# Attention's per-head steps at fixed distances, all gates of branch A in pairs, and seven projection tiles of branch B behind the last head

## The chip, the cores and the metric

The kernel runs on one core of one Trainium2 chip. Its engines are named in the profile as PE (TensorE matmul) with PEld (TensorE weight load), DVE (VectorE), ACT (ScalarE), POOL (GpSimd) and SP (SyncE, which here only issues DMA transfers). The metric is the device time of one execution in microseconds (us), lower is better; several runs are taken and the median is compared. Profiles come from one further execution.

## The reference, cut to what matters

One layer for 512 frames of width 2048, all in float32. Two mixers share one projection of the normalised input; their outputs are projected, gated and summed.

```python
h = rmsnorm(x, norm_gain)
proj = h @ w_in
(aq, ak, av, az, iq, ik, iw, rq, rk, rv, rz, ga, gb) = jnp.split(proj, SPLIT_POINTS, axis=-1)
...
a_out = dsa_mixer(aq, ak, av, iq, ik, iw, positions, rel_bias) * jax.nn.silu(az)
...
b_out = retention_mixer(rq, rk, rv, ret_gn_gain) * jax.nn.silu(rz)
merged = jax.nn.sigmoid(ga) * (a_out @ w_a_out) + jax.nn.sigmoid(gb) * (b_out @ w_b_out)
r = x + merged @ w_o
return r + (p_i @ w_ple) * jax.nn.sigmoid(r @ w_ple_gate)
```

Mixer A is attention of 8 heads of 128 channels, in which each frame sees a chosen set of up to 128 keys and a bias by distance. Mixer B is a retention of 8 heads. The widths of `az` and `rz` are 1024 each (8 tiles of 128 channels), those of `ga` and `gb` 2048 each (16 tiles).

## The kernel before

**Numbers in two parts.** TensorE multiplies float32 operands rounded to a shorter form (`fp32r`). To keep float32 accuracy every operand is split into a high part and the rest: ScalarE rounds (`wh`, `hh`, `akh`: L138, L386, L673), VectorE or GpSimd subtracts (`wl`, `hl`, `akl`: L144, L387, L674). A product is then three matmuls, high by high, high by low, low by high (`gemms`, L198 to L200). Channels lie on the 128 partitions, the 512 frames along the free axis.

**Steps.** The order of the work is written out by hand. TensorE's program is a chain of steps, one `step()` behind each group of matmuls (three in `gemms` and `values`, two in `gemm_pair`). All other work is queued to be emitted at a step: `later(n, f)` puts `f` n steps ahead of the present one; `todo` is a list of which one entry is taken at each step, in order, so that what is added to a list that is not yet empty comes later; `bg` is background work, of which one entry is taken at every `rate`-th step in which `todo` gives nothing. Each engine executes its own instructions in the order in which they are emitted, and waits in that order.

**Weights.** Each block of 8 rows of 128 weights is a unit: loaded by SP into one of 7 `wraw` buffers (L117), rounded by ScalarE (`wh`), subtracted (`wl`). `split_to` is called at the first step of a unit and emits the splits of units up to 3 ahead, `load_to` the loads of units up to 8 ahead. `pool_units` (L330, L331) lists the ranges of units of which GpSimd instead of VectorE makes `wl`; the second covers attention from its first head to the end of the single gate tiles.

**Pairs.** `gemm_pair` makes two tiles of 128 output channels at once, from 7 products of half size instead of 8 (`PRODUCTS`, L213). Its inputs are 56 prepared tiles `Xh`, loaded from DRAM. A product of a pair is 8 steps of one matmul of 512 and one of 256 columns, so a pair is 56 steps of two matmuls. `gate_pair` applies the gate's function and stores the result.

**Stages around the change**, in order: retention; pairs for `rz` (4), `gb` (8), `ga` (8) and the first four heads of `az` (2, `AZ_PAIRED`); during the last of these B's gated output is loaded and split into `bparts` (`b_load`, L882), from 20 empty steps on, one head every four steps. Then 16 tiles of branch B's output projection (L902 to L907), gated and stored in `mbs`, during which x is loaded again and split into `hparts` (`x_again`). Then attention: a values projection (`values`, 64 steps) ahead of heads 0 and 4, and for each head a queries tile and a keys tile of 16 steps each. Then four single gate tiles (`gated`, L1028) for heads 4 to 7, and branch A's output projection (L1043 to L1053), which needs `aparts`, the gated heads in two parts.

**A head** (`attention_head`, L913) loads its bias and adds the mask on GpSimd at its start (`bm`, L916, L917), projects queries and keys and splits them, and puts the rest on `todo`: the split of the values, four `logits` steps (matmuls, then VectorE adds the bias and takes the maximum), `exps` on ScalarE, `normalize` on VectorE, eight `turn` steps of two 32x320 transposes each on VectorE (L709), two `turn` steps of ScalarE (`pth`, L976) and two of VectorE (`ptl`, L978), and four `outs` steps of matmuls (L992), after which ScalarE copies the head's output `oT`. This list has 38 entries, and a head's two tiles have 32 steps. Heads 0 to 3 are gated during heads 4 to 7 (`a_kept`, L1008).

**Memory.** Tiles of 128 x 512 come from 65 slots (`U`), those of 128 x 1280 (`bm`, `pn`, `pth`, `ptl` among them) from 5 (`B`). A new tile takes the slot that has been free longest and waits for that slot's last reader.

Of the kernel before, what the change touches and what calls it, by code (L numbers as in the profile page):

```python
# [34 lines left out]
def block_kernel(tc, xT, pT, posb, posq, w_in, w_v, w_ik, w_a, w_b, w_o, w_ple, w_gate,  # L35
# [4 lines left out]
    with contextlib.ExitStack() as ctx:  # L40
# [39 lines left out]
        def block(src, chunks, cols=128):  # L80
            ids, k0 = [], 0
            for nk in chunks:
                ids.append(len(units))
                units.append((raw(src, k0, nk, cols), None, nk, cols))
                k0 += nk
            return ids

        def block_pair(s1, s2):

            b11, b12, b21, b22 = (s1, 0), (s2, 0), (s1, 8), (s2, 8)
            first = len(units)
# [83 lines left out]
        def drain():  # L177
            while todo or soon:
                step()
# [135 lines left out]
        u_rz = [block_pair(col(RZ, h), col(RZ, h + 1)) for h in range(0, NH, 2)]  # L315
        u_gb = [block_pair(col(GB, m), col(GB, m + 1)) for m in range(0, 16, 2)]
        u_ga = [block_pair(col(GA, m), col(GA, m + 1)) for m in range(0, 16, 2)]
        u_az = [block_pair(col(AZ, h), col(AZ, h + 1)) for h in range(0, AZ_PAIRED, 2)]
        u_wb = [block(w_b[m], (8,)) for m in range(16)]
        u_a, u_av = [], []  # L320
        for h in range(NH):
            if h % 4 == 0:
                u_av.append(block(w_v[2 + h // 4], (2,) * 8, 512))
            u_a.append([block(col(g, h), K8) for g in (AQ, AK)])
        u_az += [block(col(AZ, h), K8) for h in range(AZ_PAIRED, NH)]
        PAIRED = [m + 8 * i for m in range(8) for i in range(2)]
        u_wa = {m: block(w_a[m], (8,)) for m in PAIRED}
        u_d = [block_pair(w_o[m], w_o[m + 8]) for m in range(8)]
        u_p = [block(w_ple[:, 8 * q:8 * q + 8], (8,)) for q in range(MF // 4)]
        pool_units.append((u_r[0][0][0] + 4, u_r[-1][1][-1] + 1))  # L330
        pool_units.append((u_a[0][0][0] + 4, u_a[-1][1][-1] + 9))  # L331
        u_e = [block(w_gate[m], K8) for m in range(MF)]
        u_t = block(w_gt[0], (2,) * 4 + (1,) * 8, 512), block(w_pt[0], (1, 1), 512)

# [334 lines left out]
        def split(src, name, lag=0):  # L669

            h = U(name + "h", F32R)
            l = U(name + "l", F32R)
            later(lag, lambda: act.activation(h, src, AF.Copy))  # L673
            later(lag and lag + 1, lambda: dve.tensor_sub(l, src, h.bitcast(F32)))  # L674
            return h, l
# [201 lines left out]
        for us, dst in ((u_gb, sgb), (u_ga, sga)):  # L877
            for n, u in enumerate(us):
                gate_pair(u, AF.Sigmoid, to(dst[2 * n:2 * n + 2]))
        bparts = []  # L880

        def b_load(h):  # L882
            t = U("bk")
            sp.dma_start(t, bd[h])
            later(4, lambda: bparts.append(split(t, "b")))

        for n in range(AZ_PAIRED // 2):
            if n == AZ_PAIRED // 2 - 1:
                todo.extend([None] * 20)
                for h in range(NH):  # L890
                    todo.extend([lambda h=h: b_load(h)] + [None] * 3)
            gate_pair(u_az[n], AF.Silu, to(zd[2 * n:2 * n + 2]))
# [6 lines left out]

        state["rate"] = 2  # L900
        todo.extend([f for k in range(KT) for f in (lambda k=k: x_again(k), None, None, None)])
        for m in range(16):  # L902
            s = U("sg")
            sp.dma_start(s, sgb[m])
            pw = gemm(u_wb[m], bparts, "ps_w")
            dve.tensor_mul(s, pw, s)
            later(4, lambda m=m, s=s: sp.dma_start(mbs[m], s))  # L907
        drain()


        oTs = []

        def attention_head(h, vs):  # L913
            hc = slice(128 * (h % 4), 128 * (h % 4) + 128)
            bm = B("bm")
            sp.dma_start(bm, scr[h])  # L916
            pool.tensor_add(bm, bm, mneg)  # L917
            ps = gemm(u_a[h][0], hparts, "ps_aq")
            q = U("aq")
            dve.scalar_tensor_tensor(q, ps, 128.0 ** -0.5, R["b"], op0=OP.mult, op1=OP.mult)  # L920
            qs = split(q, "aq", 1)
            ps = gemm(u_a[h][1], hparts, "ps_ak")
            k = U("ak")
            dve.tensor_mul(k, ps, R["b"])
            ks = split(k, "ak", 1)
            mx = S("mx", 4)
            sums = S("sums", 4)
            E = {}

            def logits(t):  # L930
                ln = 128 * (t + 1)
# [51 lines left out]
            def outs(n):  # L983
                if n == 0:
                    E["po"] = P("ps_o")
                po = E["po"]
                for i in range(3 * n, min(3 * n + 3, len(seq))):
                    a, b, j = seq[i]
                    if j == NT - 1:
                        pe.matmul(po[:, 384:], vs[j][:, hc], bm[:, 896:1024], start=False, stop=False)  # L990
                    else:
                        pe.matmul(po[:, 128 * j:], E["v"][a][:, tok(j)], E["p"][b][:, JOFF[j]:JOFF[j] + L - 128 * j],  # L992
                                  start=(i == 0), stop=(i == len(seq) - 1))
                if n == 3:
                    oT = U("oT")
                    act.activation(oT, po, AF.Copy)
                    oTs.append(oT)
# [8 lines left out]
        aparts = [None] * NH  # L1006

        def a_kept(h):  # L1008
            z = U("z")
            sp.dma_start(z, zd[h])  # L1010
            later(24, lambda: dve.tensor_mul(z, z, oTs[h]))

            def parts():
                aparts[h] = split(z, "a")

            later(25, parts)

        for h in range(NH):
            if h % 4 == 0:
                state["rate"] = 1  # L1020
                av = values(u_av[h // 4], "av")
                while bg:
                    bg.popleft()()
            if h >= NH - AZ_PAIRED:
                a_kept(h - NH + AZ_PAIRED)
            attention_head(h, av)

        def gated(uz, o):  # L1028
            ps = gemm(uz, hparts, "ps_z")
            z = U("z")  # L1030
# [233 lines left out]
AHEAD = 4  # L1264
LOADS = 5
BG_RATE = 3
BG_RATE2 = 24
X_AHEAD = 10
AZ_PAIRED = 4
WARM = 10  # L1270
MANUAL = True

# [95 lines left out]
```

## Time and profile before

| | us |
|---|---|
| median of 3 runs | 1810.67 |
| lowest and highest of them | 1810.29, 1814.06 |
| the profiled execution, its own time | 1809.38 |
| its span, from the first to the last instruction | 1807.6 |

Its granted TensorE clock is 0.990 of full speed over the span. In the profile a row of a group or a timeline names the line, the engine, the operation and `out<-in` by the program's names, then shapes and a count. The idle time shown beside it is that of the same engine just ahead of the instruction, with the instruction that ended it. Where each stage lies, by the first start of its matmuls:

| stage | from, us |
|---|---|
| pairs of gates | 404.1 |
| 16 tiles of branch B's projection | 874.0 |
| values projection, then heads 0 to 3 | 973.0, 1026.8 |
| values projection, then heads 4 to 7 | 1128.9, 1178.3 |
| four single gate tiles | 1284.9 |
| 16 tiles of branch A's projection | 1346.6 |
| pairs of the last projection, w_o | 1433.7 |

### The profile page before, as it was taken

Reading aid. Unit: us, or ns where it says so; the run is one execution under the profiler, and the core shown is the slowest. Engines: PE = TensorE matmul, PEld = TensorE weight load, DVE = VectorE, ACT = ScalarE, POOL = GpSimd, SP = SyncE. Lnnn points to the kernel's source line nnn. Section 1 sums busy time; section 2 is a strip of 40 time slices with the busy share of each in tenths; the row PEclk is TensorE's granted clock in tenths of the full one; section 3 lists DMA queues with packets and bytes.
Section 4 is the critical chain, followed back from the end, with each engine's and each line's share of the span. In section 5 each row is a group of like instructions: output and inputs, shape, how many; then the busy total and the mean of one; then the engine's idle time right before and its main releaser. Section 6 shows DMA issues by size and latency. Waiting matters only on the chain. (4 is left out here: it accounts for less than half of the span.)

```text
span 1807.6 us, 23881 instructions
## 1 busy us (share of the span) xinstructions
PE 1752.1 (97%) x8966; PEld 1462.5 (81%) x8966; DVE 1210.6 (67%) x1959; ACT 738.1 (41%) x1087; POOL 395.4 (22%) x262
## 2 busy tenths in 40 slices
PE   9999999998999999999999999998989999999997
PEld 7988788887888888888777777886778888878887
DVE  8787874867776667776765357547557878774453
ACT  7464332224444545444532333333334443463332
POOL 2002344432321111110000144354310011111222
PEclk9999999999999999999999999999999999999999
DMA  7327652389878877778875423333236578753312
GB/s 280 110 101 265 227 189 98 102 286 290 231 196 208 209 201 206 201 198 202 295 251 178 135 96 104 106 108 117 71 107 206 161 212 205 174 175 105 94 59 93
DMA packets 114580, 309.65 MB, mean 171 GB/s; under 512 B 12832, under 2 KB 21024, under 8 KB 114464
## 3 DMA queue, kind: packets, MB, share of 16 engines
q1 hardware_dynamic: 91072, 244.15, 40.1%
q0 software_dynamic: 13600, 49.29, 14.7%
q10 hardware_dynamic: 9792, 14.68, 2.4%
q8 instruction: 70, 1.15, 0.3%
q14 instruction: 46, 0.38, 0.1%
HBM read 266.14 MB, written 41.94 MB: 170 GB/s over the span
## 5 line engine op out<-in xcount | busy, mean ns | idle before, releaser
L138 ACT ACTIVATE wh<-wraw 128x1024 fp32r<-128x1024 f32 (+2 forms) x404 | 415.5, 1043 | 535.3 <-issue 100.0
L144 DVE TENSOR_TENSOR wl<-wraw,wh 128x1024 fp32r<-128x1024 f32 (+2 forms) x324 | 401.7, 1243 | 258.7 <-ACT wh L138 258.3
L144 POOL TENSOR_TENSOR wl<-wraw,wh 128x1024 fp32r<-128x1024 f32 x80 | 192.6, 2410 | 339.8 <-ACT wh L138 243.2
L106 POOL DMA_DIRECT2D wraw<-w_in x66 | 58.9, 955 | 366.9 <-DVE wl L144 255.3
L253 PE MATMUL ps_r<-hs,wh 128*128 128x512 f32 x352 | 127.9, 402 | 3.7 <-DVE e_d L232 3.4
L694 PE MATMUL ps_vn<-wh,hh 128*128 128x512 f32 x256 | 102.1, 399 | 0.0
L695 PE MATMUL ps_vn<-wl,hh 128*128 128x512 f32 x256 | 100.1, 391 | 0.0
L696 PE MATMUL ps_vn<-wh,hl 128*128 128x512 f32 x256 | 99.8, 390 | 0.0
L254 PE MATMUL ps_r<-hs,wl 128*128 128x256 f32 x352 | 99.0, 281 | 0.2 <-DVE wl L144 0.2
L253 PEld LDWEIGHTS ps_r<-hs,wh 128*128 128x128 f32 x352 | 66.0, 188 | 23.9 <-issue 8.2
L198 PE MATMUL ps_pg<-rh,wh 128*128 128x512 f32 x192 | 74.7, 389 | 0.0
L199 PE MATMUL ps_pg<-rl,wh 128*128 128x512 f32 x192 | 74.7, 389 | 0.0
L200 PE MATMUL ps_pg<-rh,wl 128*128 128x512 f32 x192 | 74.7, 389 | 0.0
L254 PEld LDWEIGHTS ps_r<-hs,wl 128*128 128x128 f32 x352 | 66.5, 189 | 1.1 <-DVE wl L144 1.0
L106 POOL DMA_DIRECT2D wraw<-w_o x24 | 21.1, 933 | 206.8 <-DVE wl L144 179.2
L709 DVE STREAM_TRANSPOSE bm<-pn 32x320 f32<-32x320 f32 x128 | 64.3, 503 | 1.9
L253 PE MATMUL ps_v<-hs,wh 128*128 128x512 f32 x176 | 65.0, 407 | 0.0
L253 PE MATMUL ps_v<-ha,wh 128*128 128x512 f32 x176 | 63.7, 397 | 0.0
L253 PE MATMUL ps_q<-ha,wh 128*128 128x512 f32 x176 | 63.3, 399 | 0.0
L253 PE MATMUL ps_p<-hs,wh 128*128 128x512 f32 x176 | 63.3, 398 | 0.0
L253 PE MATMUL ps_p<-ha,wh 128*128 128x512 f32 x176 | 63.3, 399 | 0.0
L917 POOL TENSOR_TENSOR bm<-bm,mneg 128x1280 f32<-128x1280 f32 x8 | 21.7, 2708 | 182.1 <-DMA bm<-scr 182.1
(389 smaller groups left out, 4709.3 us busy)
## 6 DMA issues: line engine op xcount, KB each, us to landing
wraw<-w_in SPq DMA_DIRECT2D x174, 512.0 KB, 4.4
wraw<-w_in POOLq DMA_DIRECT2D x66, 512.0 KB, 7.9
wraw<-w_v SPq DMA_DIRECT2D x32, 512.0 KB, 3.9
wraw<-w_o SPq DMA_DIRECT2D x32, 512.0 KB, 4.3
wraw<-w_o POOLq DMA_DIRECT2D x24, 512.0 KB, 7.7
wraw<-w_gate SPq DMA_DIRECT2D x24, 512.0 KB, 4.3
hd<-hs SPq DMA_DIRECT2D x32, 256.0 KB, 2.4
hs<-hd SPq DMA_DIRECT2D x32, 256.0 KB, 5.9
```

What stands on the lines that cost most here:

```text
L106: pool.dma_start(out=raw_tiles[r], in_=src[:, k0:k0 + 8, :], accum_op=OP.add)
L138: act.activation(h, raw, AF.Copy)
L144: e.tensor_sub(l, raw, h.bitcast(F32))
L198: pe.matmul(o, h[:, k, w], a, start=(s == order[0]), stop=False)
L199: pe.matmul(o, h[:, k, w], b, start=False, stop=False)
L200: pe.matmul(o, l[:, k, w], a, start=False, stop=(s == order[-1]))
L253: pe.matmul(o, h[:, k], x, start=(n < 4 and k == 0), stop=False, skip_group_check=True)
L254: pe.matmul(o[:, LO], l[:, k], x[:, LO], start=False, stop=(k == 7), skip_group_check=True)
L694: pe.matmul(pss[t], a[:, tok(t)], h[:, k], start=(s == 0), stop=False)
L695: pe.matmul(pss[t], a[:, tok(t)], l[:, k], start=False, stop=False)
L696: pe.matmul(pss[t], b[:, tok(t)], h[:, k], start=False, stop=(s == KT - 1))
L709: dve.transpose(out=d[32 * a:32 * a + 32, :, 32 * b:32 * b + 32], in_=f[32 * b:32 * b + 32, :, 32 * a:32 * a + 32])
```

## The change

All eight heads of `az` are made in pairs (2 pairs more), and the four single gate tiles are gone. Branch B's projection makes nine tiles (`WB_FIRST`) ahead of attention and seven behind head 7's keys. As `bparts` has to give its room to attention, each of its 16 tiles is also stored to DRAM by SP (`bp_d`) once it is split, and loaded again during head 7's keys (`b_again`). The loads of B's output start after 12 empty steps instead of 20. A head's steps no longer stand on `todo`: each is set with `later` at a fixed distance from the end of its keys. Its bias is loaded 11 steps into its queries. Each head is gated by itself (`gate`), 34 and 46 steps behind its keys. The background rate in the pairs is 20 instead of 24. The range of GpSimd's `wl` now ends with the seven moved tiles.

```diff
-        u_az = [block_pair(col(AZ, h), col(AZ, h + 1)) for h in range(0, AZ_PAIRED, 2)]
-        u_wb = [block(w_b[m], (8,)) for m in range(16)]
+        u_az = [block_pair(col(AZ, h), col(AZ, h + 1)) for h in range(0, NH, 2)]
+        u_wb = [block(w_b[m], (8,)) for m in range(WB_FIRST)]
...
-        u_az += [block(col(AZ, h), K8) for h in range(AZ_PAIRED, NH)]
+        u_wb += [block(w_b[m], (8,)) for m in range(WB_FIRST, 16)]
...
-        pool_units.append((u_a[0][0][0] + 4, u_a[-1][1][-1] + 9))
+        pool_units.append((u_a[0][0][0] + 4, u_a[-1][1][-1] + 17 - WB_FIRST))
...
         bparts = []
+        bp_d = dp.tile([2 * NH, 128, L], F32, name="bpd")
 
         def b_load(h):
             t = U("bk")
             sp.dma_start(t, bd[h])
-            later(4, lambda: bparts.append(split(t, "b")))
-
-        for n in range(AZ_PAIRED // 2):
-            if n == AZ_PAIRED // 2 - 1:
-                todo.extend([None] * 20)
+
+            def parts():
+                bparts.append(split(t, "b"))
+                later(4, lambda: [sp.dma_start(bp_d[2 * h + i], b.bitcast(F32)) for i, b in enumerate(bparts[h])])
+
+            later(4, parts)
+
+        for n in range(NH // 2):
+            if n == NH // 2 - 1:
+                todo.extend([None] * 12)
                 for h in range(NH):
                     todo.extend([lambda h=h: b_load(h)] + [None] * 3)
...
-        for m in range(16):
+
+        def project_b(m):
             s = U("sg")
             sp.dma_start(s, sgb[m])
             pw = gemm(u_wb[m], bparts, "ps_w")
             dve.tensor_mul(s, pw, s)
-            later(4, lambda m=m, s=s: sp.dma_start(mbs[m], s))
+            later(4, lambda: sp.dma_start(mbs[m], s))
+
+        for m in range(WB_FIRST):
+            project_b(m)
         drain()
-
-
-        oTs = []
+        bparts.clear()
+
 
         def attention_head(h, vs):
             hc = slice(128 * (h % 4), 128 * (h % 4) + 128)
-            bm = B("bm")
-            sp.dma_start(bm, scr[h])
-            pool.tensor_add(bm, bm, mneg)
+            E = {}
+
+            def bias():
+                E["bm"] = B("bm")
+                sp.dma_start(E["bm"], scr[h])
+                pool.tensor_add(E["bm"], E["bm"], mneg)
+
+            later(11, bias)
...
+            if h == NH - 1:
+                for i in range(NH):
+                    later(2 * i + 2, lambda i=i: b_again(i))
             ps = gemm(u_a[h][1], hparts, "ps_ak")
+            bm = E["bm"]
...
-            todo.extend([None] * 2 + [values_split])
-            todo.extend([lambda t=t: logits(t) for t in range(NT)])
-            todo.extend([exps] + [None] * 6 + [normalize])
-            todo.extend([None] + [lambda i=i: turn(i) for i in range(8)] + [None] * 4)
-            todo.extend([lambda i=i: turn(i) for i in range(8, 12)] + [None, None])
-            todo.extend([lambda n=n: outs(n) for n in range(4)])
...
+            def gate(i):
+                if i == 0:
+                    E["z"] = U("z")
+                    sp.dma_start(E["z"], zd[h])
+                elif i == 1:
+                    dve.tensor_mul(E["z"], E["z"], E["oT"])
+                else:
+                    aparts.append(split(E["z"], "a", 1))
+
+            for t in range(NT):
+                later(4 + t, lambda t=t: logits(t))
+            later(9, exps)
+            later(12, values_split)
+            later(16, normalize)
+            for i, n in enumerate((18, 20, 21, 23, 24, 26, 27, 29, 32, 34, 35, 37)):
+                later(n, lambda i=i: turn(i))
+            for n in range(4):
+                later(41 + n, lambda n=n: outs(n))
+            for i, n in enumerate((34, 46, 46)):
+                later(n, lambda i=i: gate(i))
+
+        aparts = []
+
+        def b_again(i):
+            t = [U(n, F32R) for n in ("bh", "bl")]
+            for j in range(2):
+                sp.dma_start(t[j].bitcast(F32), bp_d[2 * i + j])
+            bparts.append(t)
...
-            if h >= NH - AZ_PAIRED:
-                a_kept(h - NH + AZ_PAIRED)
             attention_head(h, av)
-
-        def gated(uz, o):
-            ps = gemm(uz, hparts, "ps_z")
-            z = U("z")
-            dve.tensor_mul(z, ps, R["b"])
-            later(1, lambda: act.activation(z, z, AF.Silu))
-            later(2, lambda: pool.tensor_mul(z, z, o()))
-            return split(z, "a", 4)
-
-        for h in range(AZ_PAIRED, NH):
-            aparts[h] = gated(u_az[h - AZ_PAIRED // 2], lambda h=h: oTs[h])
+        for m in range(WB_FIRST, 16):
+            project_b(m)
         drain()
...
-BG_RATE2 = 24
+BG_RATE2 = 20
 X_AHEAD = 10
-AZ_PAIRED = 4
+WB_FIRST = 9
```

More of the change, by code (lines that the diff above doesn't have):

```diff
@@ L927, in attention_head @@
             sums = S("sums", 4)
-            E = {}
             def logits(t):
@@ L994, in outs @@
                 if n == 3:
-                    oT = U("oT")
-                    act.activation(oT, po, AF.Copy)
-                    oTs.append(oT)
-            todo.extend([None] * 2 + [values_split])
-            todo.extend([lambda t=t: logits(t) for t in range(NT)])
-            todo.extend([exps] + [None] * 6 + [normalize])
-            todo.extend([None] + [lambda i=i: turn(i) for i in range(8)] + [None] * 4)
-            todo.extend([lambda i=i: turn(i) for i in range(8, 12)] + [None, None])
-            todo.extend([lambda n=n: outs(n) for n in range(4)])
-        aparts = [None] * NH
-        def a_kept(h):
-            z = U("z")
[L1010 to L1016, printed above, removed]
+                    E["oT"] = U("oT")
+                    act.activation(E["oT"], po, AF.Copy)
+            def gate(i):
[23 more added lines that the diff above has]
+            bparts.append(t)
         for h in range(NH):
@@ L1023, in block_kernel @@
                     bg.popleft()()
-            if h >= NH - AZ_PAIRED:
-                a_kept(h - NH + AZ_PAIRED)
             attention_head(h, av)
-        def gated(uz, o):
-            ps = gemm(uz, hparts, "ps_z")
-            z = U("z")
-            dve.tensor_mul(z, ps, R["b"])
-            later(1, lambda: act.activation(z, z, AF.Silu))
-            later(2, lambda: pool.tensor_mul(z, z, o()))
-            return split(z, "a", 4)
-        for h in range(AZ_PAIRED, NH):
-            aparts[h] = gated(u_az[h - AZ_PAIRED // 2], lambda h=h: oTs[h])
+        for m in range(WB_FIRST, 16):
+            project_b(m)
         drain()
```

## The prediction

> **What bounds the kernel now.** I read the page first, then the busy time in stretches cut at the stage borders, then the waits of TensorE, and last the order of time on each engine at two places that the change touches.
>
> ```profile
> span 1807.6 us, 23881 instructions
> PE 1752.1 (97%) x8966; PEld 1462.5 (81%) x8966; DVE 1210.6 (67%) x1959; ACT 738.1 (41%) x1087; POOL 395.4 (22%) x262
> ```
>
> TensorE is busy nearly all the time, so the time can only come from fewer matmul columns, from TensorE's idle time, or from its clock. The stretches below (start:end, span, busy time of PE, PEld, DVE, ACT, POOL with counts, granted clock, DMA share, GB/s) are: heads 0 to 3, second values projection, heads 4 to 7, four single gate tiles. The waits under them are those of that whole stage, and then those around the entry into branch B's projection (line, waited for, us in total, times, longest).
>
> ```profile
> 1025.50:1126.00 100.50, 96.52 (x434) 78.88 (x433) 56.52 (x106) 36.35 (x67) 42.42 (x18) 1.00 0.31 104
> 1126.00:1179.00 53.00, 53.00 (x243) 44.04 (x242) 27.88 (x57) 18.32 (x30) 22.51 (x10) 1.00 0.30 102
> 1179.00:1284.00 105.00, 98.76 (x433) 80.77 (x432) 63.58 (x107) 35.22 (x67) 47.29 (x20) 0.97 0.31 105
> 1284.00:1346.40 62.40, 54.94 (x229) 44.40 (x228) 38.95 (x70) 23.01 (x35) 16.27 (x8) 0.92 0.27 88
> ...
> PE ps_o L992 <- ACT pth L976: 10.4, 9, 4.9
> PE ps_o L992 <- DVE ptl L978: 6.8, 6, 4.3
> PE ps_l L679 <- DVE akl L674: 0.5, 2, 0.3
> ...
> PE ps_w L199 <- DVE bl L674: 0.7, 2, 0.5
> PE ps_w L198 <- ACT bh L673: 0.4, 1, 0.4
> ```
>
> The attention stage loses 10.4 + 6.8 + 0.5 = 17.7 us to waits, nearly all for the turned probabilities (`pth`, `ptl`) ahead of `outs`. The clock costs 0.03 x 105 = 3.2 and 0.08 x 62.4 = 5.0 us more, 8.2 together. So 25.9 us is all that new distances could win there. The entry into branch B's projection waits 1.1 us for its split input.
>
> **The change part by part: matmuls.** Rows of three tiles (count, ns min/median/max, first and last start):
>
> ```profile
> L198 PE MATMUL ps_w<-ah,wh x128: 389/389/389, 1346.6 to 1433.0; 128*128 128x512 f32 x128
> L253 PE MATMUL ps_q<-ma,wh x64: 391/396/403, 1440.1 to 1583.5; 128*128 128x512 f32 x64
> L253 PE MATMUL ps_q<-ha,wh x176: 391/395/504, 419.8 to 861.6; 128*128 128x512 f32 x176
> ```
>
> A step of three full matmuls takes (1433.0 - 1346.6) / 127 = 0.680 us. The four single gate tiles are 4 x 16 = 64 steps, 43.5 us; they go. In a pair the third product's first and last start lie 7 pairs and 7 steps apart in the w_o stage: at about 0.35 us a step, (143.4 - 2.5) / 7 = 20.1 us a pair. The gate pairs, with masks and bias matmuls between, take (441.8 - 2.5) / 21 = 20.9. Two more cost 40.3 to 41.8, so 1.7 to 3.2 us are won; I take **-2.5**. Seven of branch B's tiles (8 steps each) move as they are: 56 x 0.680 = 38.1 us go in one place and come back in the other, **0**. What follows head 7's keys is now 56 steps instead of 64; its last new step stands at distance 48, so the cover suffices. If head 7's chain ran more than 8 + 7 steps (10 us) late, the first w_a tile would wait for it.
>
> **Attention.** What decides is when VectorE ends the 16 transposes of a head (after `normalize`), against the next head's keys. Head 0 into head 1, in order of time (start, us, engine, line, what, idle before):
>
> ```profile
> 1048.74 0.69 DVE L924 TENSOR_TENSOR ak<-ps_ak,r_b 128x512 f32<-128x512 f32 x1 [7.03 <-PE ps_ak L200]
> 1050.18 2.48 DVE L674 TENSOR_TENSOR akl<-ak,akh 128x512 fp32r<-128x512 f32 x1 [0.74 <-ACT akh L673]
> 1066.78 7.23 DVE L709 STREAM_TRANSPOSE bm<-pn 32x320 f32<-32x320 f32 x14
> 1077.77 0.69 DVE L674 TENSOR_TENSOR akl<-ak,akh 128x512 fp32r<-128x512 f32 x1 [0.70 <-ACT akh L673]
> ...
> 1048.56 1.06 ACT L138 ACTIVATE wh<-wraw 128x1024 fp32r<-128x1024 f32 x1 [4.38 <-PE ps_ak L199]
> 1049.53 0.61 ACT L673 ACTIVATE akh<-ak 128x512 fp32r<-128x512 f32 x1
> 1074.11 1.36 ACT L976 ACTIVATE pth<-bm 128x512 fp32r<-128x512 f32 x2 [5.80 <-DVE bm L709]
> 1075.38 1.04 ACT L138 ACTIVATE wh<-wraw 128x1024 fp32r<-128x1024 f32 x1
> ...
> 1049.70 2.40 POOL L144 TENSOR_TENSOR wl<-wraw,wh 128x1024 fp32r<-128x1024 f32 x1 [0.45 <-ACT wh L138]
> ```
>
> The subtraction `akl` takes 0.69 us alone and 2.48 beside POOL's `wl`: it ends 0.55 us behind POOL's end (1052.10). The transposes run back to back until 1074.0, so VectorE, not the list of steps, sets their end; spacing them wider doesn't bring it forward. Now the new distances. Head 1's keys end 32 steps behind head 0's (1048.5): 21.8 us, and some 2 us of head 0's own small matmuls, so at 1072.4. Its second logits, the first that need `akl`, are issued 5 steps later, at 1076.0. On ScalarE the first half of `pth` stands at distance 32, which is ahead of the weight unit's `wh` and of `akh`: 1074.1 + 0.7, then 1.04 (to 1075.8), then 0.61 (to 1076.4). POOL's `wl` runs 1075.8 to 1078.2, `akl` ends at 1078.7, and TensorE has waited 2.7 us. Before, the list held these logits back behind `turn` and `outs`, so the same lateness showed in front of `outs` instead. So the stall is not removed; it moves from `outs` to the logits, and it comes at every head that follows another directly: 1, 2, 3, 5, 6, 7.
>
> From the second head of each four on, the gate of the head before falls into the same stretch; before, only heads 4 to 7 carried such work. Its rows in the stretch 1179 to 1284 (count, busy, mean ns):
>
> ```profile
> L674 DVE TENSOR_TENSOR al<-z,ah 128x512 fp32r<-128x512 f32 x4 | 6.3, 1582 | 5.7 <-ACT ah L673 5.6
> L1011 DVE TENSOR_TENSOR z<-z,oT 128x512 f32<-128x512 f32 x4 | 4.0, 1010 | 0.1
> ```
>
> That is 2.6 us of VectorE ahead of the transposes, partly in idle time; I let half of it, 1.3, reach the end. Then the keys' own multiplication comes late too and the first logits wait: 2.7 + 1.3 = 4.0 us a head. Sum: heads 0 and 4, which follow a values projection, 0.25 each (the 0.5 of the row, two times); heads 1 and 5, 2.7; heads 2, 3, 6, 7, 4.0; 1 us for `outs`: 22.9. The least is 8 x 0.25 = 2, if transposes end in time; the most about 38, if the 2.6 us of the gate, and POOL's bias addition (moved into the same stretch, 11 steps into the next head), count whole at each. With the clock as before (8.2) that is 31.1 against 25.9: **+5**, from -22 to +20.
>
> The rows tie the clock to stalls: 0.97 and 0.92 where the waits of 4.9 and 4.3 us lie, 1.00 in the stretch of heads 0 to 3, whose waits are shorter. By the Trainium skill (TensorE: Matmul & The Clock Gate, "Why this matters for your kernels") one idle window of some 3 us takes the clock to half, and shorter gaps between bursts don't; by that rule alone stalls of 2.7 to 4.0 us, cut by a matmul or two, would lie about its border, and a sum in which none of them halves the clock is 8.2 us less.
>
> **The entry into branch B's projection.** Each split head of B is now also stored, from SP's queue, in the order load, load, store pair, load, store pair. A store waits for `bl`, and all that SP has to issue behind it waits too.
>
> ```profile
> bk<-bd SPq DMA_DIRECT2D x8, 256.0 KB, 4.5
> ...
> SPq L272 <- DVE ha L268: 58.0, 14, 8.5
> ...
> 860.67 0.43 SPq L884 DMA_DIRECT2D bk<-bd  x1
> 864.79 0.86 SPq L884 DMA_DIRECT2D bk<-bd  x2
> ...
> L673 ACT ACTIVATE bh<-bk x8: 616/632/636, 867.3 to 879.4; 128x512 fp32r<-128x512 f32 x8
> L674 DVE TENSOR_TENSOR bl<-bk,bh x8: 683/688/694, 868.0 to 880.1; 128x512 fp32r<-128x512 f32 x8
> L198 PE MATMUL ps_w<-bh,wh x128: 387/389/505, 874.0 to 971.6; 128*128 128x512 f32 x128
> ```
>
> The second row shows that such a store (of the same kind, in `combos`) holds SP up to 8.5 us. Now the load of head h+2 is issued only when head h is split and its stores are out: 2 x 0.43 + 0.43 for the issues, 4.5 to land, 0.63 for `bh`, 0.69 for `bl`, 0.3 between, 7.4 us a link. Three links lead from head 0 to head 6. Head 0's `bl` starts at 868.0 now; eight fewer empty steps (2.8 us) bring it to 865.2 at best, say 866.6, done at 867.3. Then head 6 is split at 889.5. TensorE reaches it at 874.0 + 6 x 0.68 = 878.1: 11.4 us late, 10.3 net of the 1.1 waited before. ScalarE and VectorE stand at the loads in between, so the `wl` queued behind them are late as well, inside the same wait. If head 0 is split at its place in the list (862) it is 5 net; if the loads ran ahead, 0; with slower landings beside 4 MB of stores, 14. I take **+8**, and a clock drop behind it, priced as those two of the last stretch (5.0 / 2), **+2.5**.
>
> **At nothing:** the reload of 16 split tiles during head 7's keys (0 to +4): slots come free two a step, one pair is asked for every second step, and the first is used 14 steps (9.5 us) behind its load against 4.5 to land. SP's own issues, 16 x 0.43, lie in 32 steps, with weights loaded nine units ahead; without that cover the first moved tiles wait. The rate of the background work (24 to 20) and the shorter first part of B move some masks later (-1 to +2):
>
> ```profile
> L629 PE MATMUL ps_bias<-mk,d x384: 219/304/390, 502.8 to 1013.4; 128*32 128x128 bf16 x48, 128*32 128x256 bf16 x48, 128*32 128x384 bf16 x48, 128*32 128x512 bf16 x48
> ```
>
> They end 13 us before head 0's queries (1026.8), which is the room for them.
>
> **Sum:** -2.5 + 5 + 8 + 2.5 = **+13** on the profiled execution's 1809.4 (span 1807.6 and 1.8 around it); that execution lies 1.3 under the runs' median of 1810.7. On the median: **1823**.
>
> **The rivals.** *Stalls vanish (faster).* Place: the six transitions between heads. If the transposes end before the first `pth` is due at distance 32, and `akh` gets past ScalarE ahead of them, only the 0.25 a head remains: 25.9 goes to about 3, so -2.5 - 23 + 10.5 = -15, 1796. It decides as soon as the transposes end 2 us earlier. For it: 12 steps are given to them instead of 8, and the row of 14 leaves little else between. Against: the same row, back to back until 1074.0. *The clock stays up (little slower).* Stalls as forecast, none long enough: 8.2 less, 1815. For it: the 1.00 of heads 0 to 3. Against: 2.7 and 1.3 lie close together. *The spill is hidden anyway (no change).* SP and the splits run ahead in idle slots: -2.5 + 5 - 1.1, 1812. Against: 868.0 is late already. *Both worse (slower).* Entry 14 and 2.5, and 6 us more at the heads' stalls and clock than the forecast's 5: -2.5 + 11 + 16.5 = +25, 1836. For it: 2.6 us of gate work at each head, beside POOL's.
>
> **How the numbers follow.** Forecast 0.42, stalls vanish 0.17, clock stays up 0.10, spill hidden 0.14, both worse 0.17. A measurement tells about 0.2% from no change, 1807 to 1814.3. Faster: 0.17 and 0.04 of the hidden spill, 0.21. Same: 0.08 of that and half the clock case, 0.13. Slower: the rest, 0.66. The range runs from the vanished stalls to just over the worse case, 1795 to 1840; the forecast's own is 1815 to 1830.
>
> **What would show it.** In the waits of TensorE: `ps_l` for `akl` or `ak` at six heads, some 3 us each, and `ps_o` nearly gone; `ps_w` for `bl` or `wl` 5 to 12 us at the entry; SP waiting at the new store for `bl`; 24 pairs at 20 to 21 us. I'm wrong in the main thing if attention's waits fall under 10 us, or if the entry waits under 3.

## The result and the profile after

| | before | after |
|---|---|---|
| median of 5 runs of each, us | 1811.84 | 1824.15 |
| lowest and highest of them | 1810.29, 1817.65 | 1817.19, 1826.02 |
| profiled execution, and its span | 1809.38, 1807.6 | 1817.19, 1815.4 |
| granted clock over the span | 0.990 | 0.987 |

The ratio is 1.0054 with an interval of 1.0031 to 1.0078: slower, by 12 us between the medians. The profiled execution of after is the shortest of its five, so the two profiles differ by only 7.8 us. First the head of the page after, then TensorE's waits (line, waited for, us in total, times, longest) and SP's at the new store.

```profile
span 1815.4 us, 24108 instructions
PE 1751.9 (97%) x8998; PEld 1464.9 (81%) x8998; DVE 1220.2 (67%) x1986; ACT 743.2 (41%) x1096; POOL 396.0 (22%) x263
```

```profile
PE ps_l L679 <- DVE akl L674: 12.7, 8, 2.1
PE ps_r L253 <- DVE e_d L232: 10.9, 12, 5.8
...
PE ps_bias L629 <- DVE mk L621: 3.9, 1, 3.9
...
PE ps_l L953 <- DVE ak L942: 3.2, 2, 1.6
...
PE ps_l L678 <- ACT akh L673: 1.4, 6, 0.3
...
PE ps_w L198 <- ACT bh L673: 0.7, 1, 0.7
...
SPq L889 <- ACT bh L673: 14.2, 7, 5.4
```

`ps_o` is gone from the list. In its place stand the three rows of `ps_l`: 12.7 + 3.2 + 1.4 = 17.3 us, against 17.7 for `outs` and logits together before. New are one wait of 5.8 us for `e_d` and one of 3.9 us for a mask. TensorE's busy time is the same on both pages (1752.1 and 1751.9).

**Where the time went, by stage.** The rows of these tiles give each stage's border (duration min/median/max, first and last start):

```profile
L253 PE MATMUL ps_p<-ha,wh x192: 389/398/774, 403.0 to 896.0; 128*128 128x512 f32 x192
...
L198 PE MATMUL ps_w<-bh,wh x128: 389/389/792, 922.0 to 1354.7; 128*128 128x512 f32 x128
...
L198 PE MATMUL ps_aq<-hh,wh x128: 387/389/628, 1041.5 to 1297.4; 128*128 128x512 f32 x128
...
L198 PE MATMUL ps_w<-ah,wh x128: 389/389/389, 1355.4 to 1441.8; 128*128 128x512 f32 x128
```

| from one first start to the next | before | after | what is moved in or out | net |
|---|---|---|---|---|
| `ps_p` to B's `ps_w`: pairs | 469.9 | 519.0 | two pairs come, 2 x 20.9 | +7.3 |
| B's `ps_w` to `ps_aq`: projection, values | 152.8 | 119.5 | seven tiles go, 38.1 | +4.8 |
| `ps_aq` to A's `ps_w`: attention | 319.8 | 313.9 | gate tiles go, 43.5; seven tiles come, 38.1 | -0.5 |

The last column is after less before, with the moved work taken out. With 1.7 us won by the exchange of 43.5 for 41.8, 1.1 ahead of the pairs and 1.0 behind attention, this gives 11.6 - 3.8 = 7.8 us. Attention gained nothing, and the entry into branch B's projection cost some 12 us on both sides of its first matmul. The same differences, taken out in the same way, serve for all the experiments below.

**Attention.** Between head 0 and head 1, in order of time (start, us, engine, line, what, idle before):

```profile
1083.92 7.22 DVE L709 STREAM_TRANSPOSE bm<-pn 32x320 f32<-32x320 f32 x14
1091.17 0.69 DVE L942 TENSOR_TENSOR ak<-ps_ak,r_b 128x512 f32<-128x512 f32 x1
1093.37 2.42 DVE L674 TENSOR_TENSOR akl<-ak,akh 128x512 fp32r<-128x512 f32 x1 [1.50 <-ACT akh L673]
...
1091.23 0.63 ACT L993 ACTIVATE pth<-bm 128x512 fp32r<-128x512 f32 x1 [7.34 <-DVE bm L709]
1091.77 1.04 ACT L138 ACTIVATE wh<-wraw 128x1024 fp32r<-128x1024 f32 x1
1092.72 0.61 ACT L673 ACTIVATE akh<-ak 128x512 fp32r<-128x512 f32 x1
...
1092.89 2.35 POOL L144 TENSOR_TENSOR wl<-wraw,wh 128x1024 fp32r<-128x1024 f32 x1 [6.53 <-ACT wh L138]
```

The row of 14 transposes ends at 1091.14, ScalarE runs `pth`, `wh`, `akh`, GpSimd takes up `wl` once `wh` is there, and `akl`, released 0.5 us later, lasts 2.42 us instead of 0.69. That is the order which the prediction wrote down. The rows of `akl` before and after show how general it became: two of the slow kind among eight (heads 0 and 4, which follow a values projection and lose 0.2 to 0.3 us each), then all eight.

```profile
L674 DVE TENSOR_TENSOR akl<-ak,akh x8: 691/692/2483, 1050.2 to 1291.7; 128x512 fp32r<-128x512 f32 x8
...
L674 DVE TENSOR_TENSOR akl<-ak,akh x8: 2418/2423/2473, 1064.9 to 1312.9; 128x512 fp32r<-128x512 f32 x8
```

**The entry.** Its start, on SP, ScalarE and VectorE:

```profile
906.42 0.33 SPq L889 DMA_DIRECT2D bpd<-bh  x1
...
909.01 0.38 SPq L889 DMA_DIRECT2D bpd<-bl  x1
909.49 0.42 SPq L885 DMA_DIRECT2D bk<-bd  x1
...
914.86 0.63 ACT L673 ACTIVATE bh<-bk 128x512 fp32r<-128x512 f32 x1 [3.79 <-DMA bk<-bd]
...
915.52 0.69 DVE L674 TENSOR_TENSOR bl<-bk,bh 128x512 fp32r<-128x512 f32 x1 [2.60 <-ACT bh L673]
916.13 0.68 DVE L232 TENSOR_TENSOR e_d<-ps_r,pv 128x512 f32<-128x512 f32 x1
...
930.75 0.94 SPq L903 DMA_DIRECT2D xk<-xT  x2
...
937.62 0.72 ACT L386 ACTIVATE hh<-xk,g_sb 128x512 fp32r<-128x512 f32 x1 [4.61 <-DMA xk<-xT]
...
938.38 0.75 DVE L387 SCALAR_TENSOR_TENSOR hl<-xk,g_sb,hh 128x512 fp32r<-128x512 f32 x1 [4.31 <-ACT hh L386]
939.04 0.35 DVE L621 TENSOR_SCALAR mk<-relf,thr 128x256 bf16<-128x256 f32 x1
```

SP stands at the stores until a head is split (`bh`, then `bl`), and only then issues the next load; that of the fourth head of B goes out at 909.49. ScalarE idles 3.79 us for this load, VectorE 2.60 us for ScalarE, and right behind this `bl` stands `e_d`, which the last product of the last pair needs (the 5.8 us). The lateness travels on: SP comes to the loads of x only at 930.75, VectorE idles 4.31 us at `hl`, and behind it stands the mask (the 3.9 us). TensorE never had to wait long for `bl` itself, since it was already late at these other places.

### The profile page after: what moved, and what is told of

The parts are those of the page before. It is cut to its first block, busy times and chain, and to the rows that moved or that the text cites. A ratio compares the mean times of both kernels' runs of the same rounds, so it can differ in the third digit from the quotient of the medians.

```text
span 1815.4 us, 24108 instructions
## 1 busy us (share of the span) xinstructions
PE 1751.9 (97%) x8998; PEld 1464.9 (81%) x8998; DVE 1220.2 (67%) x1986; ACT 743.2 (41%) x1096; POOL 396.0 (22%) x263
## 5 line engine op out<-in xcount | busy, mean ns | idle before, releaser
L144 DVE TENSOR_TENSOR wl<-wraw,wh 128x1024 fp32r<-128x1024 f32 (+2 forms) x331 | 408.1, 1236 | 256.0 <-ACT wh L138 255.3
L253 PE MATMUL ps_r<-hs,wh 128*128 128x512 f32 x384 | 142.1, 408 | 8.9 <-DVE e_d L232 8.6
L254 PE MATMUL ps_r<-hs,wl 128*128 128x256 f32 x384 | 108.9, 284 | 0.1
L253 PEld LDWEIGHTS ps_r<-hs,wh 128*128 128x128 f32 x384 | 73.2, 191 | 31.0 <-issue 7.3
L254 PEld LDWEIGHTS ps_r<-hs,wl 128*128 128x128 f32 x384 | 73.6, 192 | 0.9 <-DVE wl L144 0.9
L253 PE MATMUL ps_v<-hs,wh 128*128 128x512 f32 x192 | 70.9, 407 | 0.0
L253 PE MATMUL ps_p<-ha,wh 128*128 128x512 f32 x192 | 69.5, 401 | 0.0
L253 PE MATMUL ps_p<-hs,wh 128*128 128x512 f32 x192 | 69.3, 399 | 0.1
L253 PE MATMUL ps_q<-ha,wh 128*128 128x512 f32 x192 | 69.2, 400 | 0.0
L857 ACT ACTIVATE go<-go 128x512 f32<-128x512 f32 x48 | 30.0, 625 | 75.3 <-DVE go L854 75.2
```

Source lines behind the costliest of these rows:

```text
L144: e.tensor_sub(l, raw, h.bitcast(F32))
L253: pe.matmul(o, h[:, k], x, start=(n < 4 and k == 0), stop=False, skip_group_check=True)
L254: pe.matmul(o[:, LO], l[:, k], x[:, LO], start=False, stop=(k == 7), skip_group_check=True)
```

## The experiments

Ratios are to the kernel before, run on the same chip in the same turn; its median there was 1799.0 to 1802.2.

**e1. The stores issued 36 instead of 4 steps behind the split.**

```diff
-                later(4, lambda: [sp.dma_start(bp_d[2 * h + i], ...
+                later(36, lambda: [sp.dma_start(bp_d[2 * h + i], ...
```

> The changed kernel, in which the 16 stores of branch B's split tiles are emitted 36 instead of 4 steps behind their split, so that on SP's queue all eight loads lie ahead of all stores. Theory (a store on SP waits for its split and holds the loads behind it, and VectorE stands at those loads): the waits at the entry (5.8 us for e_d in the last pair, 3.9 us for a mask, 0.9 us for bh and bl in the changed kernel's profile) fall from 10.6 to under 3 us and the two half-clock stretches there go, so 8 to 15 us less than the changed kernel's 1824: 1809 to 1816. Rival (the 4 MB of stores crowd the loads wherever they stand): the waits stay over 7 us and the time within 4 us of 1824.

Measured 1.0026 (1.0010 to 1.0042). Two of TensorE's waits:

```profile
PE ps_r L253 <- DVE e_d L232: 5.3, 6, 2.1
...
PE ps_bias L629 <- DVE mk L621: 5.1, 3, 2.8
```

The 5.8 us ahead of the projection are gone, the masks wait longer than in the changed kernel (5.1 us for 3.9): at 36 steps the stores fall among the loads of x on SP. About 5 us were won, less than the 8 expected at least; the load chain is a cause, and the place of the stores was badly chosen. e7 and e11 move them further.

**e2. The keys split at once, not one step later.** So ScalarE's `akh` gets ahead of the weight unit's `wh`, and GpSimd starts later.

```diff
-            ks = split(k, "ak", 1)
+            ks = split(k, "ak")
```

> The changed kernel, in which the keys of a head are split at once instead of one step later, so that on ScalarE akh stands ahead of the weight unit's wh, and akl is subtracted before GpSimd starts on that unit. Theory (the logits wait for akl because wh and GpSimd's 2.4 us come first): the waits of ps_l for akl fall from 12.7 us to under 3, those for the keys themselves (ak, 3.2 us at heads 1 and 5) stay, and of the four half-clock stretches in attention at least two go; 10 to 16 us less than 1824: 1808 to 1814. Rival (the transposes alone make the logits late, whatever the order behind them): the wait moves to ak or akh and the time stays within 4 us of 1824.

Measured 0.992 (0.9902 to 0.9938), more than expected. The row of `akl`, then what is left of attention's waits:

```profile
L674 DVE TENSOR_TENSOR akl<-ak,akh x8: 692/693/695, 1059.5 to 1289.2; 128x512 fp32r<-128x512 f32 x8
...
PE ps_l L953 <- DVE ak L942: 4.8, 6, 1.6
```

Attention's stage fell from 275.8 to 255.8 us. The waits explain 12.5 of the 20; the remaining 7.5 go with the clock, 0.97 over this stage in the changed kernel and 1.00 here, where TensorE is busy 8.0 us less with the same 1132 matmuls:

```profile
1041.50:1317.30 275.80, 258.46 (x1132) 211.93 (x1132) 159.35 (x300) 92.38 (x167) 120.02 (x48) 0.97 0.37 120
```

```profile
1036.10:1291.90 255.80, 250.50 (x1132) 206.15 (x1131) 162.24 (x299) 92.85 (x167) 120.50 (x48) 1.00 0.37 129
```

(Columns: start:end, span, busy time of PE, PEld, DVE, ACT, POOL, granted clock, DMA share, GB/s.)

**e3. The edits of e1 and e2 together.**

> Both edits: late stores and keys split at once. Theory: the two stalls lie in different stages and add up, 18 to 30 us less than 1824: 1794 to 1806, below the kernel before (1812). Rival (they hide the same delay, or what is won is lost again further on): no more than the better one of the two.

Measured 0.9911 (0.9896 to 0.9927), within the interval of e2. By the ratios that is 26 us under the changed kernel, in the theory's range, but e2 alone had already won 24, so this doesn't show that the two add up. The masks still waited 3.8 us, so late stores of this kind add little that can be told.

**e4. The kernel before, with attention's fixed distances and the later bias alone** (no spill, no pairs for heads 4 to 7).

```diff
-            todo.extend([None] * 2 + [values_split])
...
+            for t in range(NT):
+                later(4 + t, lambda t=t: logits(t))
...
+            for i, n in enumerate((18, 20, 21, 23, 24, 26, 27, 29, 32, 34, 35, 37)):
+                later(n, lambda i=i: turn(i))
```

> The kernel before, with the fixed distances and the later bias load of attention's steps alone; gates, branch B's projection and everything else as before. Theory (the stall only moves from outs to the logits): the waits of ps_o (17.2 us) fall under 4, those of ps_l rise from 0.5 to 14 to 20, and the time is within 5 us of the kernel before, 1807 to 1817. Rival (the distances win and other parts of the change lose it): 8 us or more below the kernel before. Second rival (the list's slack was worth more): 6 us or more above.

Measured 1.0008 (0.9995 to 1.0021).

```profile
PE ps_l L679 <- DVE akl L674: 11.3, 8, 2.1
PE ps_l L941 <- DVE ak L930: 7.5, 4, 3.7
...
PE ps_l L678 <- ACT akh L673: 1.1, 3, 0.6
```

That is 19.9 us at the logits for 17.2 at `outs` and 0.5 at the logits, and no `ps_o`. The distances alone move the stall and win nothing.

**e5. The changed kernel, with attention back on the list** (the gate's steps 1 and 2 steps behind `outs`).

```diff
-            for t in range(NT):
-                later(4 + t, lambda t=t: logits(t))
...
+            todo.extend([None] * 2 + [values_split])
+            todo.extend([lambda t=t: logits(t) for t in range(NT)])
```

> The changed kernel, with attention's steps back on the list in the old order and the gate of a head one and two steps behind its outs; all pairs, the stores, the reload and the seven moved tiles stay. Theory (the distances are worth nothing in sum, the entry costs 0.5%): ps_l waits under 3 us, ps_o waits 15 to 25 us again, the waits at the entry as in the changed kernel (over 8 us), ratio to the kernel before 1.003 to 1.010. Rival (the distances cost the time): ratio under 1.001.

Measured 1.0061 (1.0042 to 1.0081), the changed kernel's own ratio. Attention takes 275.7 us, with its stall again at `outs`:

```profile
PE ps_o L1010 <- ACT pth L994: 11.4, 6, 5.0
...
PE ps_o L1010 <- DVE ptl L996: 4.7, 5, 3.2
```

**e6. The transposes on consecutive steps.** If spacing them set their end, it would show here.

```diff
-            for i, n in enumerate((18, 20, 21, 23, 24, 26, 27, 29, 32, 34, 35, 37)):
+            for i, n in enumerate((17, 18, 19, 20, 21, 22, 23, 24, 32, 34, 35, 37)):
```

> The changed kernel, with the eight transposing steps at distances 17 to 24, one a step, instead of spread over 18 to 29; all else as there. Theory (VectorE executes them back to back, so the spacing in the list doesn't set their end): ps_l waits within 3 us of the changed kernel's 17.3, ratio to the kernel before 1.002 to 1.008. Rival (the wide spacing itself makes them late): ps_l waits under 12 us and a ratio under 1.001.

Measured 1.0059 (1.0038 to 1.0080). The waits for `akl` and `ak` are 12.1 and 7.2 us, and none for `akh` is left: 19.3 us against 17.3, with the increase at the `ak` of heads 1 and 5 (3.6 us each for 1.6). Attention takes 276.9 us instead of 275.8. The spacing is worth a microsecond at most; the same stage differs by as much between the changed kernel, e1 and e11.

**e7. The keys split at once, and the stores issued behind the loads of x.**

```diff
-                later(4, lambda: [sp.dma_start(bp_d[2 * h + i], ...
+                later(104 - 2 * h, lambda p=bparts[h]: [sp.dma_start(bp_d[2 * h + i], ...
...
-            ks = split(k, "ak", 1)
+            ks = split(k, "ak")
```

> The changed kernel with the keys split at once, and the 16 stores behind the loads of x (76 to 90 steps later than in the late-store kernels' first), so that neither the loads of branch B's output nor those of x stand behind a store on SP. Theory (with the stores late, the wait for a mask behind the split of x, 3.8 to 5.1 us, was SP held by stores among the x loads): that wait falls under 1 us, and the ratio to the kernel before is 0.985 to 0.990, against 0.991 with both edits. Rival (4 MB more of transfers crowd the loads anyway): the wait stays and the ratio is 0.990 to 0.993.

Measured **0.9886** (0.9863 to 0.9910), the fastest of all, ahead of both kernels: 1780.0 us beside 1799.0. The mask's wait is 0.7 us:

```profile
PE ps_r L253 <- DVE e_d L232: 6.6, 9, 2.1
...
PE ps_bias L629 <- DVE mk L621: 0.7, 1, 0.7
```

**e8. The kernel before with the fixed distances of e4 and the keys split at once.**

```diff
+            for t in range(NT):
+                later(4 + t, lambda t=t: logits(t))
...
-            ks = split(k, "ak", 1)
+            ks = split(k, "ak")
```

> The kernel before, with the fixed distances, the later bias load and the keys split at once; two pairs of az and four single gate tiles, no stores, no moved tiles. Theory (the stalls of attention are the order on ScalarE and GpSimd, and pairs with the spill win nothing net): ps_l waits for akl under 2 us, of the 7.5 us for ak most stays at heads 4 to 7, ratio 0.986 to 0.992, at or under that of the changed kernel with the keys split at once (0.992). Rival (the pairs are worth having): ratio over 0.995.

Measured 0.9931 (0.9906 to 0.9956), a little short of what was expected: 8.7 us of waits for `ak` are left, the longest 3.7. Attention comes to 262.6 us net of the gate tiles. The rest of the change, with its stores placed well (e7), stands 0.45% below this: the longest of e7's four runs (1782.7 us) is shorter than the shortest of these six (1783.1).

**e9. The keys split late, as in the change, but VectorE makes the `wl` that would meet `akl`.** Eight units are taken from GpSimd, their subtraction four steps later.

```diff
-                e = pool if nk * cols == 1024 and any(a <= i < b for a, b in pool_units) else dve
+                e = pool if nk * cols == 1024 and any(a <= i < b for a, b in pool_units) and i not in at_keys else dve
...
-                later(1 if e is dve else 2, rest)
+                later(4 if i in at_keys else 1 if e is dve else 2, rest)
```

> The changed kernel, with the order on ScalarE as there (pth, wh, akh), but the low part of the one weight unit whose split falls on the end of a head's keys is made by VectorE, four steps later and so behind akl, instead of by GpSimd; eight units in all. It tells the two halves of the akl wait apart. Theory (akl takes 2.4 instead of 0.7 us because GpSimd's operation runs): the waits of ps_l for akl fall from 12.7 to 1 to 4 us, akl takes 0.69 us, and the ratio to the kernel before is 0.993 to 1.000. Rival (the 1.04 us of wh ahead of akh is the larger half): the akl waits stay over 7 us and the ratio is over 1.001.

Measured 0.995 (0.993 to 0.997).

```profile
1085.99 0.69 DVE L675 TENSOR_TENSOR akl<-ak,akh 128x512 fp32r<-128x512 f32 x1 [1.50 <-ACT akh L674]
...
PE ps_l L680 <- DVE akl L675: 2.1, 6, 0.3
```

The `akh` is as late as in the change (1.50 us of idle time ahead of `akl`), and still the wait for `akl` falls from 12.7 to 2.1 us, since the subtraction takes 0.69 us. So GpSimd's operation beside it is the larger part of that stall, and ScalarE's order the smaller.

**e10. The kernel before with the keys split at once, and nothing else.**

```diff
-            ks = split(k, "ak", 1)
+            ks = split(k, "ak")
```

> The kernel before with the keys split at once, its attention still on the list. Theory 'the two go together': on the list the logits already stand behind the transposes and their akl took 0.69 us in head 1, so there is nothing for the early split to win; the waits for pth and ptl ahead of outs stay at 15 to 18 us, and the ratio to before is 0.998 to 1.003. Rival 'the split alone does it': the waits fall under 8 us, and the ratio is 0.994 or less, near that of the distances and the early split together (0.993).

Both were wrong: 1.0062 (1.0041 to 1.0082), slower. The waits at `outs` grew from 17.2 to 27.5 us:

```profile
PE ps_o L992 <- DVE ptl L978: 14.6, 7, 4.3
PE ps_o L992 <- ACT pth L976: 12.9, 9, 5.8
...
1104.53 5.46 DVE L978 TENSOR_TENSOR ptl<-bm,pth 128x512 fp32r<-128x512 f32 x2 [0.77 <-ACT pth L976]
...
1104.05 5.12 POOL L144 TENSOR_TENSOR wl<-wraw,wh 128x1024 fp32r<-128x1024 f32 x2 [8.18 <-ACT wh L138]
```

Now, at heads 1 and 5, it is the pair of `ptl`, 1.69 us where nothing runs beside it, that lies beside GpSimd and takes 5.46 and 5.45; the waits there account for 9 of the 10 us. On the list, `outs` follows right behind `ptl`; at the fixed distances there is room for it (35 and 37 against 41): in e2 a `ptl` beside `wl` takes 2.70 us instead of 0.95, and no `outs` waits. So the early split needs the distances, and the distances need the early split: neither wins alone (1.0062 and 1.0008), both together give 0.9931.

**e11. The changed kernel with the stores of e7 alone.**

```diff
-                later(4, lambda: [sp.dma_start(bp_d[2 * h + i], ...
+                later(104 - 2 * h, lambda p=bparts[h]: [sp.dma_start(bp_d[2 * h + i], ...
```

> The changed kernel with its stores issued behind the loads of x, the keys split as in the change. Theory 'the entry costs some 14 us (8 ahead of branch B's projection, 6 behind it), and attention nothing': the entry's waits for e_d and the masks fall to about 3 us, attention keeps its 17 us of waits for the keys, and the ratio to before is 0.996 to 1.000, 0.006 to 0.009 under that of the changed kernel. Rival 'the gain with the early split was all attention's': the ratio stays at 1.002 or more.

Measured 0.9991 (0.9974 to 1.0007), 0.0063 under the changed kernel, with its waits in attention unchanged (12.7, 3.2 and 1.4) and 0.4 us left at the masks. This is the cost of the entry by itself: 11 us, where 14 were expected.

**The stages of all runs.** Each is the profiled execution's, between the same first starts, with the moved work taken out as in the table above (41.8 us of pairs, 38.1 of tiles, 43.5 of gate tiles):

| kernels | pairs | projection and values | attention |
|---|---|---|---|
| before's pairs and projection: before, e4, e8, e10 | 469.9, 460.8, 463.2, 462.6 | 152.8, 152.6, 154.7, 154.7 | 276.3, 279.9, 262.6, 288.0 |
| stores 4 steps behind: after, e2, e5, e6, e9 | 477.2, 472.2, 474.2, 466.5, 470.8 | 157.6, 155.4, 157.2, 155.7, 155.6 | 275.8, 255.8, 275.7, 276.9, 259.3 |
| stores 36 steps behind: e1, e3 | 468.3, 460.5 | 157.6, 155.4 | 277.6, 255.5 |
| stores behind x: e7, e11 | 464.1, 466.7 | 149.9, 149.5 | 257.3, 276.5 |

One stage of one execution can be off by several us (before's own pairs lie 9.1 above the same pairs in e4), but the means tell the parts apart. Stores at 4 steps cost 472.2 - 464.1 = 8.1 us in the pairs and 156.3 - 153.7 = 2.6 behind, 10.7 in all. The division between the two is less sure than the sum: at the background rate of 20, 36 more of the bias matmuls (`ps_bias`, 144 instead of 108) fall among the pairs, 1.5 us of TensorE's busy time that the first row doesn't have there. Beside the last row, which has them too, the same stores cost 472.2 - 465.4 = 6.8 and 156.3 - 149.7 = 6.6. Attention stands at 276 to 280 when the keys are split late, on the list or at distances, and at 256 to 263 when `akl` is freed of GpSimd at fixed distances; e10 has 288.

## Why the prediction was right, and where it was off

**The sum.** +13 on the profiled execution and 1823 on the median were forecast; 1824.15 came, and +7.8 between the two profiles. By the means above the entry gives 10.7, the exchange of gate tiles for pairs -1.7 and attention nothing, 9.0 in all, which agrees with the 9.8 us of the ratio (0.0054 x 1811.84). That the median came within 1.2 us of the forecast is therefore partly luck: of the +13, the 10.5 for the entry held in sum, the +5 for attention didn't.

**The entry** is the term that came true: +8 and +2.5 in the prediction, 8.1 and 2.6 by the means over runs (6.8 and 6.6 beside the kernels with the stores behind x), 11 by e11. That 8.1 and 2.6 match term by term is chance: the +2.5 was to be a clock drop, which did come (0.97 behind the first `ps_w` after, 1.00 before: 0.03 x 119.5 = 3.6 us), but the 3.9 us of the mask stood in no term. The mechanism, loads queued behind stores on SP that wait for the split, is shown by SP's 14.2 us at the new store and by e11. Its place was not as written. "`ps_w` for `bl` or `wl` 5 to 12 us" did not come: those waits are 0.9 us. VectorE stood behind the loads as forecast, but `e_d` and the masks are in its queue too, and these TensorE needs sooner. The step that failed named only `wl` as queued behind the waiting split. The chain was also quicker: `bl` of head 6 started at 925.21 and that of head 0 at 906.42, so three links took 18.8 us, not 22.2.

**Attention: the mechanism was right, the size wrong.** The prediction's main step, "the stall is not removed; it moves from `outs` to the logits", is what e4 and e5 show from both sides. The mis-sized term is "heads 2, 3, 6, 7, 4.0": the 1.3 us that half of the gate's work was to add. The trace has 2.3 us at each of these four heads (2.1 for `akl`, 0.2 for `akh`). In the changed kernel `gate` stands at 34 and 46 steps, which is 2 and 14 behind the next head's keys; there VectorE idles 5.2 us ahead of the values' split, the gate's two operations of 0.68 us each come behind that, and still no wait for `ak` follows at these heads. What came late instead is `ak` at heads 1 and 5 (two waits of 1.6 us, so 4.0 and 3.8 us there for the 2.7 forecast). VectorE ahead of head 1's keys, then the same multiplication ahead of head 2's, then GpSimd:

```profile
1076.02 1.79 DVE L963 TENSOR_TENSOR avl<-av,avh 128x128 fp32r<-128x128 f32 x3 [4.51 <-ACT avh L961]
1077.93 3.55 DVE L981 TENSOR_SCALAR pn<-bm,ri 128x128 f32<-128x128 f32 x4
...
1108.54 1.59 DVE L981 TENSOR_SCALAR pn<-bm,ri 128x128 f32<-128x128 f32 x4
...
1074.61 2.65 POOL L929 TENSOR_TENSOR bm<-bm,mneg 128x1280 f32<-128x1280 f32 x1
1077.70 2.39 POOL L144 TENSOR_TENSOR wl<-wraw,wh 128x1024 fp32r<-128x1024 f32 x1 [0.45 <-ACT wh L138]
```

The split of the values (`avl`) and the multiplications of `normalize` (`pn`) lie beside GpSimd's bias addition and the `wl` behind it, and `pn` takes 2.0 us more than ahead of head 2. So the transposes start late, and `ak` behind them. Ahead of head 5 it is the same (`pn` 3.63). The prediction had the bias addition only in its upper bound. So the sum was 17.3 us, not 22.9, and with the clock (0.03 x 107.5 + 0.05 x 107.9 = 8.6, against the 8.2 taken) attention came out at 25.9, as before: 0 in place of +5.

```profile
1041.50:1149.00 107.50, 101.02 (x440) 82.88 (x440) 63.91 (x122) 36.14 (x67) 47.73 (x19) 0.97 0.34 107
...
1201.00:1308.90 107.90, 101.60 (x440) 83.22 (x439) 64.02 (x121) 34.67 (x66) 50.26 (x20) 0.95 0.47 153
```

**"Spacing them wider doesn't bring it forward"** is borne out by e6: a microsecond at most.

**The pairs.** "24 pairs at 20 to 21 us" is about right: (896.0 - 403.0 - 2.5) / 23 = 21.3. The reload of the 16 tiles and the moved tiles were costed at nothing, and in the two groups of late stores no row of waits speaks against it.

**The rivals.** *Stalls vanish* asked that the transposes end earlier and that `akh` gets past ScalarE, and the change does neither. e2 gains about what that rival would have (23 us forecast, 20 in the stage) with less: in head 1 the first `pth` still waits for the transposes (1085.32) and `akh` goes behind it (1085.99), but ahead of `wh` (1086.52), and that is enough. *The spill is hidden anyway* is refuted by e11. *The clock stays up* is refuted by the 0.97 and 0.95 above. By the rule of the Trainium skill (TensorE: Matmul & The Clock Gate, "Why this matters for your kernels") that was cited, one idle window of about 3 us is what halves the clock; here the longest single wait of attention is 2.1 us, and right behind head 1's waits of 1.6, 0.3 and 2.1 us, with a few matmuls between them, the granted clock is 0.51, so the trace doesn't agree, and it decides.

```profile
1095.80:1099.20 3.40, 3.36 (x10) 2.98 (x11) 2.31 (x7) 0.00 (x0) 0.00 (x0) 0.51 0.52 154
```

**What stays open.** Why the other four runs of the changed kernel take 5.6 to 8.8 us longer than its profiled one has no trace; their granted clocks (0.985 to 0.987, beside 0.987) would explain at most 0.002 x 1815 = 3.6 us. That the bias addition and the `wl` beside `pn` make `ak` late at heads 1 and 5 is read from the rows; no run moves them away, and the waits for `ak` at heads 6 and 7 of e8 (1.1 and 2.2 us) were not followed up. Versions with the stores issued from another engine's queue, or with the remaining 2.1 us at `e_d` in the last pair removed, weren't tried either.

## What to carry to other kernels

When a list is replaced by fixed distances, follow what runs beside each instruction, and not only what stands ahead of it: the same stall of 17 us sat at `outs` or at the logits, and which short subtraction lay beside GpSimd's `wl` decided its worth. Of two edits that do nothing or harm alone, both together may win, so try the pair before dropping either. A store that waits for a result is better not put ahead of loads in the same queue: this cost 11 us here, and the same stores behind the loads nothing that could be measured.

## What was not expected of the hardware

- A VectorE subtraction that starts a little after GpSimd's ends just behind it: 0.69 becomes 2.42 us for one, 1.69 becomes 5.46 for two beside two of GpSimd (5.12). The multiplications `pn` (3.55 for 1.59) were lengthened too. That it holds for `akl` and `ptl` alike, whichever comes to lie there, and so undoes a plainly good edit (e10), was not foreseen.
- Short stalls cost more than they last. In e2, 12.5 us of waits less shortened the stage by 20.0, in e9 10.6 less by 16.5, with no wait over 2.1 us among them; the clock of the stage rose from 0.97 to 1.00 in e2.
- The same stage of the same code differed by up to 10.7 us between executions (the pairs of e6 and of the changed kernel, 466.5 and 477.2), so a part's worth was only to be read from several runs.
